# A hybrid decoder layer on one core: instructions put in another order at eight places

## The chip, the core and the metric

The kernel runs on one core of a Trainium2 chip. The metric is the device time of one execution in microseconds (us), the median of several. A profile is one execution that was traced; its times are read from the span's start. PE is the matrix engine (PEld its weight loads), DVE the vector engine, ACT the scalar engine, POOL GpSimd, SP the SyncE queue, from which every transfer of this kernel is issued.

## What is computed

One layer of a decoder with 1,040 positions (16 meta tokens and 1,024 real ones) of width 1,024, all in float32. Cut to what matters:

```python
xn   = rms_norm(h, mix_pre_g)
z, xbc, dt, q, k, v = split(xn @ w_in)
xbc  = silu(causal_dwconv(xbc, conv_w, conv_b))            # 4 taps along the tokens
y_ssd = rms_norm(ssd_scan(xbc, softplus(dt + dt_bias), a_log, d_skip) * silu(z), ssd_norm_g)
y_sb  = rms_norm(stick_breaking_attention(q, k, v), sb_norm_g)   # 16 heads
h   += rms_norm(concat(y_ssd, y_sb) @ w_out, mix_post_g)
gu   = rms_norm(h, ffn_pre_g) @ w_up
h   += rms_norm((gelu(causal_dwconv3(gu[:, :F])) * gu[:, F:]) @ w_down, ffn_post_g)
return h[16:]
```

Stick-breaking attention gives each key the weight beta times the product of (1 - beta) over the keys between it and the query, a scan along the keys. The state-space scan runs over chunks of 128 tokens.

## The kernel before

Every float32 product is done as three matmuls: an operand is split into a high part (ACT copies it to the reduced format) and a low part (POOL or DVE subtracts), and high x high, high x low and low x high are summed in PSUM. Large products are cut into 2x2 blocks and done in seven products of sums (Strassen's scheme), so that DVE and POOL form sums and PE does seven of eight parts.

The stages, in order of time:

- **Head** (to about 64 us): norm of x, its turn by PE, the first projections B0 and C0.
- **Projections** (64 to 374 us): thirteen `Duo`s, each two blocks of 128 output columns: x00, z00, x02, z02, bc, x10, z10, x12, z12 (names by group and block) and qk0 to qk3. A duo is seven products of 24 matmuls each (`product`, L298 to L321). The loop over `duos` (L739) emits product `m`, then a step of splitting the next duo's weights (`split_22`, `sums`, `split_3`, `split_1`, `split_4`), then the list `slots[j]` of what is left of the previous duo. For an x duo `conv_acts` (L489) makes these: four convolution taps on DVE, Silu on ACT (L502), the skip term on ACT with its store (`skip`, L506), and the turn to token order in three parts, each a transpose on PE into one of two PSUM banks (L481, L486) and a copy on ACT (L482, L487). `done_conv` (L521) says which of these stand in which slot. `dt_acts` does the same for the step sizes.
- **V** (374 to 455 us): the value projection.
- **Scan** (455 to 620 us): 18 units, one for each chunk and group (L1158). A unit loads what later units need (`load_zx` one ahead, `load_x` two, `load_bc` three), does its matmuls, and takes steps of the fill `qk_fill` (L908), the projections of q and k for heads 8 to 15. The evacuation `ev` (L915) of such a projection writes a tile `st` that is stored to DRAM (L921). `chunk_store` stores the result `zk` (L1119). At unit 2 two blocks of V's rows are copied from DRAM to DRAM (`vcd`, L1161).
- **Attention** (620 to 925 us): 64 steps, eight blocks of queries for each of eight pairs of heads (L1530). A step loads q three steps ahead, does the scores z, the sigmoid on ACT, the scan on DVE, and turns and mixes earlier blocks. Between them `some(n)` takes fill steps within a budget. `edge_mix` (L1321) ends a pair of heads and stores its tile `ysc` (L1329).
- **Output projection** (925 to 1,106 us): for each tile of 128 tokens two chains of 24 matmuls (`out_steps`, L1451), each evacuated by DVE (`ev2`, L1996) into a tile `mb`, then the two norms (`after`) and a turn of the result by PE with its copies and subtractions (`turn_x2`, L1714).
- **Feed forward** (1,106 us to the end): up products and down products.

The order within each engine is the order in which the code emits, under `manual_schedule`: for all five queues in the head, the scan and the attention, and for PE, DVE, ACT and POOL in the rest (in the output projection from its second tile on; there SP's order is the scheduler's). So an instruction that waits holds up everything behind it on its engine. The built program gives SP's transfers eight semaphores in turn: each transfer waits, beside what it needs, until the one eight places before it has landed.

Of the kernel before, what the change touches and what calls it, by code (L numbers as in the profile page):

```python
# [67 lines left out]
def tile_layer(ctx: ExitStack, tc: tile.TileContext, x, meta, rows, parts,  # L68
# [452 lines left out]
    def done_conv(duo, blocks):  # L521
        (a, ta_), (b, tb_) = (conv_acts(*args) for args in blocks)
        return [a[:2], a[2:], b[:2], ta_[:1] + b[2:], ta_[1:2], ta_[2:], tb_[:2], tb_[2:]]

# [207 lines left out]
    def merged(*lists):  # L732
# [3 lines left out]
    dts = dt_acts()  # L736
    slots = [b0_taps[:2] + dts[0], b0_taps[2:], c0_taps[:2], c0_taps[2:] + b0_turns[:1], b0_turns[1:2], b0_turns[2:],
             dts[1]]
    for i, q in enumerate(duos):  # L739
# [26 lines left out]
        slots = q.done(q)  # L766
        for acts_ in extra:
            slots[0] = acts_ + slots[0]
        if i == 1:
            slots = merged(slots, [[], dts[2], [], [], dts[3], [], dts[4]]) + [dts[5] + dts[6]]  # L770
        if i + 1 == n_early:
            t_stack.close()
            vl = v_stack.enter_context(tc.tile_pool(name="vl", bufs=1, side="left"))
            fetch_v(1, 0, vl)
# [131 lines left out]
    left, via_sbuf = [0], [0]  # L906

    def qk_fill():  # L908
        def chain(n, qs):
            which, p = qk_blocks[n]  # L910

            def ev(acc, c0, m):
                st = st_pool.tile([P, 2, CQ], F32R, tag="st", name=f"st{which}{p}{c0}")
                nc.scalar.activation(st[:, 0, :m], acc[:, :m], AF.Copy)
                if via_sbuf[0]:  # L915
                    raw = st_pool.tile([P, CQ], F32, tag="sw", name=f"sw{which}{p}{c0}", bufs=1)
                    nc.scalar.activation(raw[:, :m], acc[:, :m], AF.Copy)
                    nc.gpsimd.tensor_tensor(st[:, 1, :m], raw[:, :m], st[:, 0, :m].bitcast(F32), op=ALU.subtract)
                else:
                    nc.vector.tensor_tensor(st[:, 1, :m], acc[:, :m], st[:, 0, :m].bitcast(F32), op=ALU.subtract)  # L920
                nc.sync.dma_start(out=qkd[p][which][:, :, c0:c0 + m], in_=st[:, :, :m].bitcast(F32))  # L921

# [16 lines left out]

    def load_k(p):  # L940
        if p < 8:
            k = qkp.tile([P, 2, L], F32R, tag="k", name=f"k{p}")
# [32 lines left out]
    with tc.tile_pool(name="ssd", bufs=1, side="right") as sp:  # L975
# [125 lines left out]
        def chunk_store(g, c, em, xdt, yt, zk, xd, between):  # L1101
# [16 lines left out]
            nc.vector.tensor_tensor(zk[:, :, ts], xd[:, :, ts], zk[:, :, ts], op=ALU.mult)  # L1118
            nc.sync.dma_start(out=yd[c][:, 4 * g:4 * g + 4, :], in_=zk[:, :, ts])  # L1119

            def square():
                if g == 0:
                    squares[c] = sp.tile([P, 8, P], F32, tag="sqk", name=f"sqk{nm}")
                nc.scalar.activation(squares[c][:, 4 * g:4 * g + 4, ts], zk[:, :, ts], AF.Square)
# [33 lines left out]
        for n, (g, c) in enumerate(units):  # L1158
            if n == 2:
                for d, u in zip(vcd, (vd, vdp)):  # L1160
# [160 lines left out]
    def edge_mix(p, th):  # L1321
# [6 lines left out]
        nc.vector.tensor_tensor(tail, av.rearrange("p (t c) -> p t c", c=32), tail, op=ALU.add)  # L1328
        nc.sync.dma_start(out=yd1[:, :, p, :].rearrange("t d c -> d t c"), in_=ysc)  # L1329
        flat = ysc.rearrange("p t c -> p (t c)")  # L1330
# [199 lines left out]
    for step in range(8 * NT):  # L1530
# [8 lines left out]

        load_q(step + 3)  # L1540
        due = mix[:1]
        if len(turn) >= TURN_LAG:
            run(begin_turn())
        block = block_weights(p, i)
        next(block, None)
# [45 lines left out]
    do(4)  # L1591
    edge_mix(7, edge)
    run(meta_steps)
    while not closed[0]:
# [389 lines left out]
    for t in range(1, NT + 1):  # L1984
# [23 lines left out]
        steps = out_steps(1, t, wres2, ys.pop(0), ev2)  # L2008
        run(steps, 2)
        run(norm, 1)  # L2010
# [426 lines left out]
```

## Time and profile before

| | us |
|---|---|
| median of 3 runs | 1765.28 |
| lowest and highest run | 1764.16, 1766.97 |
| the profiled execution | 1767.73 |
| its span in the trace | 1766.0 |
| PE busy | 1686.9 |
| DVE, ACT, POOL busy | 1095.1, 741.1, 756.8 |
| transfers of the SP queue | 245.54 MB, 43.3% of 16 engines |

The page lists for each engine the busy time, then the span in 40 slices with the clock granted to PE, the chain of work that ended last, and the costliest groups of instructions, each with the idle time before it and what ended that. The trace answers further: who waited for whom, busy times by stretch, and instructions in order of time.

### The profile page before, as it was taken

The numbers are of one execution on the slowest core, as the hardware profiler recorded it, in microseconds if no ns is written. First come the engines' busy times: TensorE is split into PE (matmuls) and PEld (weight loads), VectorE is DVE, ScalarE is ACT, GpSimd is POOL, SyncE is SP. The second block draws the span as 40 slices with busy tenths as digits, with TensorE's granted clock in tenths as the row PEclk, the third lists the DMA queues.
The fourth block names the chain that finished last, engine by engine and source line by source line (L and its number), as shares of the span: only waits on it lengthen the run. The fifth ranks groups of instructions, "written<-read, shape, count | busy, mean of one in ns | idle before, by whom it ended". The sixth has DMA issues, their size and how long they took to land.

```text
span 1766.0 us, 29016 instructions
## 1 busy us (share of the span) xinstructions
PE 1686.9 (96%) x11508; PEld 1448.5 (82%) x11508; DVE 1095.1 (62%) x1279; ACT 741.1 (42%) x1110; POOL 756.8 (43%) x591
## 2 busy tenths in 40 slices
PE   6888999999999989899999989999999999999998
PEld 5888999987767777677777777989999988888887
DVE  7747444345256678787771366676666666658777
ACT  6443333322234455565553344543333333344544
POOL 4565666711265553223232211377777767500001
PEclk8999999999999989899999999999999999999999
DMA  5342344343487764534431754223233322196335
GB/s 194 130 135 85 121 132 136 135 153 116 153 231 231 222 185 132 163 110 115 118 94 67 245 167 143 72 94 125 93 108 95 115 90 90 67 323 224 102 104 189
DMA packets 164522, 247.40 MB, mean 140 GB/s; under 512 B 18489, under 2 KB 99489, under 8 KB 162706
## 3 DMA queue, kind: packets, MB, share of 16 engines
q1 hardware_dynamic: 164386, 245.54, 43.3%
q8 instruction: 91, 1.49, 0.4%
q14 instruction: 45, 0.37, 0.1%
HBM read 162.00 MB, written 83.47 MB: 139 GB/s over the span
## 4 chain that ended last, share of the span: by engine, by line
PE 74%; DVE 6%; issue 5%; ACT 3%; DMA 2%; POOL 1%; SPq 0%; POOLq 0%; DVEq 0%; ACTq 0%
PE fX L1841 10%; PE mo L1460 7%; PE dnA L2253 7%; PE fY L1841 6%; PE fA L1841 6%; PE dnB L2253 5%; PE av L1305 3%; PE z L1266 3%; PE tw L1287 3%; PE pj_q L219 2%; PE pj_k L219 2%; PE dXqk L309 2%; PE vB L812 2%; DVE kp L1270 2%; DVE cdX L498 1%
## 5 line engine op out<-in xcount | busy, mean ns | idle before, releaser
L1270 DVE TENSOR_TENSOR_SCAN kp<-kp,hold 128x344 f32<-128x344 f32 (+6 forms) x224 | 198.6, 946 | 45.5 <-ACT kp L1267 43.3
L183 POOL TENSOR_TENSOR wlo<-wr,whi 128x1024 fp32r<-128x1024 f32 x43 | 99.3, 2318 | 42.3 <-ACT whi L182 38.8
L2290 POOL TENSOR_TENSOR fms<-fms 128x1 f32<-128x1 f32 x8 | 2.3, 288 | 222.1 <-ACT dh L2175 195.8
L182 ACT ACTIVATE whi<-wr 128x1024 fp32r<-128x1024 f32 x43 | 45.7, 1062 | 112.2 <-PE fX L1841 76.2
L1913 DVE SCALAR_TENSOR_TENSOR ga<-gr,pp,ga 128x1024 f32<-128x1024 f32 x44 | 69.3, 1575 | 34.0 <-ACT ga L1906 33.3
L2175 ACT ACTIVATE dh<-ar 128x512 fp32r<-128x512 f32 x77 | 48.6, 631 | 94.9 <-PE dnB L2253 44.7
L1267 ACT ACTIVATE kp<-z 128x688 f32<-128x688 f32 (+6 forms) x112 | 78.9, 736 | 19.5 <-PE z L1266 18.6
L1266 PE MATMUL z<-k,q 64*128 64x348 f32 (+8 forms) x672 | 78.6, 356 | 5.8 <-ACT th L1292 3.9
L1287 PE MATMUL tw<-ident,kp 128*128 128x128 f32 x576 | 77.4, 280 | 6.0 <-DVE th L1290 3.1
L2176 DVE TENSOR_TENSOR dl<-ar,dh 128x512 fp32r<-128x512 f32 x77 | 53.2, 691 | 47.0 <-ACT dh L2175 47.0
L1305 PEld LDWEIGHTS av<-th,v 128*64 128x64 f32 x1152 | 62.4, 138 | 22.5 <-issue 11.7
L1245 POOL TENSOR_SCALAR cb<-kp 128x32 f32<-128x32 f32 x64 | 37.1, 583 | 99.9 <-DVE kp L1270 99.5
L1305 PE MATMUL av<-th,v 128*64 128x128 f32 x1152 | 78.0, 280 | 0.5 <-ACT ysc L1308 0.5
L1287 PEld LDWEIGHTS tw<-ident,kp 128*128 128x128 f32 x576 | 62.7, 142 | 15.9 <-issue 6.8
L1266 PEld LDWEIGHTS z<-k,q 64*128 64x128 f32 x672 | 54.7, 195 | 23.8 <-issue 10.1
L1292 ACT ACTIVATE th<-tw 128x1024 f32<-128x1024 f32 x64 | 55.3, 864 | 33.7 <-PE tw L1287 32.2
L2253 PE MATMUL dnA<-dl,dh 128*128 128x512 f32 x176 | 68.5, 389 | 0.0
L2253 PE MATMUL dnA<-dh 128*128 128x512 f32 x176 | 68.5, 389 | 0.0
L2253 PE MATMUL dnA<-dh,dl 128*128 128x512 f32 x176 | 68.5, 389 | 0.0
L1974 POOL TENSOR_TENSOR al<-wr,ah 128x512 fp32r<-128x512 f32 x20 | 28.6, 1431 | 77.5 <-ACT ah L1973 77.4
L1460 PE MATMUL mo<-wohb,yh 128*128 128x512 f32 x128 | 51.7, 404 | 6.3 <-DVE mb L1996 6.3
L2253 PE MATMUL dnB<-dh 128*128 128x512 f32 x132 | 51.3, 389 | 0.0
(999 smaller groups left out, 6080.5 us busy)
## 6 DMA issues: line engine op xcount, KB each, us to landing
wr<-in_w_up SPq DMA_DIRECT2D x44, 512.0 KB
fds<-ga SPq DMA_DIRECT2D x44, 256.0 KB
b<-in_w_down SPq DMA_DIRECT2D x44, 256.0 KB
ar<-fds SPq DMA_DIRECT2D x44, 256.0 KB
fda<-ga SPq DMA_DIRECT2D x33, 256.0 KB
ar<-fda SPq DMA_DIRECT2D x33, 256.0 KB
k<-qkd SPq DMA_DIRECT2D x8, 1040.0 KB
q<-qkd SPq DMA_DIRECT2D x64, 128.0 KB
```

What stands on the lines that cost most here:

```text
L183: nc.gpsimd.tensor_tensor(l, raw, h.bitcast(F32), op=ALU.subtract)
L219: mm(acc[:, :CQ - s], a[:, k, :], b[:, k % 4, c + s:c + CQ], start=(k == 0 and j == 0), stop=(k == KB - 1 and j == 2))
L1266: mm(z[:, j, :w], u[h, :], r[h, a:a + w], start=s_ == 0, stop=s_ == 2)
L1267: nc.scalar.activation(kp[:, :, a:a + w], z[:, :, :w], AF.Sigmoid, scale=-QSCALE)
L1270: nc.vector.tensor_tensor_scan(part, part, hold[:, L - n + a:L - n + a + w][:, ::-1], 1.0 if ci == 0 else kp[:, j, a + w:a + w + 1], op0=A ...
L1287: nc.tensor.transpose(tw[:, j, b, :], bt[:, j, c0:c0 + P], ident)
L1292: copied[0] = nc.scalar.activation(th[:, :, :nb, :], tw[:, :, :nb, :], AF.Copy, scale=-1.0, bias=1.0).ins
L1305: mm(av[halves[j], :], v[:, kb, halves[j]], th[:, j, b, :], start=kb == 0, stop=kb == i)
L1460: recent[0] = mm(acc, u[:, k, :], v[:, cs], start=(k == 0 and j == 0), stop=(k == 7 and j == 2))
L1841: mm(acc[:, c, :nn], u[:, k, :], v[:, k, c0:c0 + nn], start=first and k == 0 and j == 0, stop=k == 3 and j == 2, skip_group_check=not first)
L1913: nc.vector.scalar_tensor_tensor(v, self.g[jj][:, :, i:i + 256], fconv_w[:, j, i:i + 1], v, op0=ALU.mult, op1=ALU.add)
L2253: mm(banks[BANK[n], t], u[:, 0, c], v[:, 1, :], start=(n in (1, 2, 5) and p == 0 and i == 0), stop=(p == NPR - 1 and i == 2), skip_group_c ...
```

## The change

Eight edits of order; no instruction is added or taken away, and POOL's order is the same.

1. `done_conv` lists a duo's Silu and skip one product later, and the turns of both blocks one product each, so that the last three turn parts of an x duo fall into the first three slots of the duo after the next. The step sizes' parts `dts` move with them, and the pool of the turned tiles closes one duo later.
2. `qk_fill`: the store of `st` is put on a list `stores` and issued at the start of the next evacuation, or by `load_k`.
3. `chunk_store`: the store of `zk` is issued with the square of the same unit, one unit later.
4. The copies `vcd` are issued at unit 12, not 2.
5. `edge_mix`: the store of `ysc` goes on the same list, and the list is emptied at step 6 of each pair too.
6. Step 0 of the attention takes its five fill steps ahead of its first scores.
7. Output projection: four steps of a tile's chains (a whole first chain with its evacuation) go ahead of the norm's steps and the turn, where there were two (half a chain).
8. The two extra slots at the end of a duo's list go to the next duo's slots 0, 1, 2 in turn, not all to slot 0.

```diff
@@ done_conv
-        return [a[:2], a[2:], b[:2], ta_[:1] + b[2:], ta_[1:2], ta_[2:], tb_[:2], tb_[2:]]
+        return [a[:2], a[2:4], a[4:] + b[:2], b[2:4], ta_[:1] + b[4:], ta_[1:2], ta_[2:], tb_[:1], tb_[1:2], tb_[2:]]
@@ first slots
-    slots = [b0_taps[:2] + dts[0], b0_taps[2:], c0_taps[:2], c0_taps[2:] + b0_turns[:1], b0_turns[1:2], b0_turns[2:],
-             dts[1]]
+    slots = [b0_taps[:2] + dts[0], b0_taps[2:4], b0_taps[4:] + c0_taps[:2], c0_taps[2:4], c0_taps[4:] + b0_turns[:1],
+             b0_turns[1:2], b0_turns[2:], dts[1]]
@@ loop over duos
-        for acts_ in extra:
-            slots[0] = acts_ + slots[0]
+        for k, acts_ in enumerate(extra):
+            slots[k] = acts_ + slots[k]
         if i == 1:
-            slots = merged(slots, [[], dts[2], [], [], dts[3], [], dts[4]]) + [dts[5] + dts[6]]
-        if i + 1 == n_early:
+            slots = merged(slots, [[], dts[2], [], dts[3], [], [], dts[4]]) + [dts[5], dts[6]]
+        if i == n_early:
@@ qk_fill, load_k
+    stores = []
+    def put_stores():
+        while stores:
+            dst, src = stores.pop(0)
+            nc.sync.dma_start(out=dst, in_=src)
             def ev(acc, c0, m):
+                put_stores()
...
-                nc.sync.dma_start(out=qkd[p][which][:, :, c0:c0 + m], in_=st[:, :, :m].bitcast(F32))
+                stores.append((qkd[p][which][:, :, c0:c0 + m], st[:, :, :m].bitcast(F32)))
     def load_k(p):
+        put_stores()
@@ chunk_store
-            nc.sync.dma_start(out=yd[c][:, 4 * g:4 * g + 4, :], in_=zk[:, :, ts])
             def square():
+                nc.sync.dma_start(out=yd[c][:, 4 * g:4 * g + 4, :], in_=zk[:, :, ts])
@@ units
-            if n == 2:
+            if n == 12:
                 for d, u in zip(vcd, (vd, vdp)):
@@ edge_mix
-        nc.sync.dma_start(out=yd1[:, :, p, :].rearrange("t d c -> d t c"), in_=ysc)
+        stores.append((yd1[:, :, p, :].rearrange("t d c -> d t c"), ysc))
@@ attention steps
         load_q(step + 3)
+        if n == 6 or (p, n) == (6, 3):
+            put_stores()
...
+        if step == 0:
+            some(5)
         block = block_weights(p, i)
@@ output projection
-        run(steps, 2)
+        run(steps, 4)
         run(norm, 1)
```

What this makes of three queues follows. First ACT in the projections, in duo z00, while x00's convolution is being finished: `cdX` is a block's Silu, `craw_x` its skip term, `craw_z` the evacuation of product 2, `whi1x` and `whi4x` the high parts of the next duo's weights, `xtkX` the copies of turned parts. Before:

```order
L502 ACTIVATE cdX_1185<-cdX_1185 128x1040
L508 ACTIVATE craw_x_841<-cdX_1185,pp 128x1040
L318 ACTIVATE craw_z_1114<-dAz_1088 128x520
L182 ACTIVATE whi1x_1251<-wrx_812 128x8x128
L487 ACTIVATE xtkX_1217<-tt_X_1_1255 128x512
L182 ACTIVATE whi4x_1286<-s24x_1149 128x8x128
L487 ACTIVATE xtkX_1217<-tt_X_2_1290 128x512
L482 ACTIVATE xtkX_1323<-tt_X_0_1324 16x128
```

The same place now:

```order
L318 ACTIVATE craw_z_1100<-dAz_1074 128x520
L182 ACTIVATE whi1x_1244<-wrx_812 128x8x128
L482 ACTIVATE xtkX_1248<-tt_X_0_1249 16x128
L502 ACTIVATE cdX_1185<-cdX_1185 128x1040
L508 ACTIVATE craw_x_841<-cdX_1185,pp 128x1040
L182 ACTIVATE whi4x_1280<-s24x_1149 128x8x128
L487 ACTIVATE xtkX_1248<-tt_X_1_1284 128x512
L487 ACTIVATE xtkX_1248<-tt_X_2_1315 128x512
```

The second block's Silu and skip have moved behind the evacuation, `whi1x` and the first turned part; `whi4x` and the other two parts still stand behind them.

Second SP in the scan at unit 2: `yd` is a unit's stored result, `vcd` the copies of V's rows, `bt`, `ct`, `bn` the state's next chunks, `zk` and `xd` what unit 3 needs, `sl` and `sg` what unit 5's decays need. Before:

```order
L1119 DMA yd_90<-zk_0_4663 128x4x2
L1161 DMA vcd_3897<-vd 8x16384
L1161 DMA vcd_3898<-vd 8x16384
L989 DMA bt_4464<-bcd_529 128x256
L990 DMA ct_4465<-bcd_530 128x256
L993 DMA bn_4466<-bnd_533 128x256
L989 DMA bt_4467<-bcd_531 128x256
L990 DMA ct_4468<-bcd_532 128x256
L993 DMA bn_4469<-bnd_534 128x256
L1028 DMA zk_1_4827<-zd_115 128x4x128
L1028 DMA xd_1_4829<-xdd_102 128x4x128
```

The same place now:

```order
L913 DMA qkd_544<-st_4729 256x1x260
L998 DMA bt_4464<-bcd_529 128x256
L999 DMA ct_4465<-bcd_530 128x256
L1002 DMA bn_4466<-bnd_533 128x256
L998 DMA bt_4467<-bcd_531 128x256
L999 DMA ct_4468<-bcd_532 128x256
L1002 DMA bn_4469<-bnd_534 128x256
L1037 DMA zk_1_4823<-zd_115 128x4x128
L1037 DMA xd_1_4825<-xdd_102 128x4x128
```

The two copies are gone from here (they stand eight and nine places ahead of `xk_7` at unit 12 now), and the store of unit 1's result has moved behind unit 2's loads.

Third DVE in the output projection, tile 4: `mb<-mo_4_0` and `mb<-mo_4_1` are the evacuations of its two chains, `b11l` and `b21l` the subtractions of tile 2's turn, `oxn` and `mo` the ends of two norms (tile 3's and that of the two last meta rows). Before:

```order
L1726 TENSOR_TENSOR b11l<-x2tp_10851,b11h 128x4x128
L1726 TENSOR_TENSOR b21l<-x2tp_10851,b21h 128x4x128
L1712 SCALAR_TENSOR_TENSOR oxn_10813<-mb_10725,rs_ff_10847,gffn 128x1024
L1712 SCALAR_TENSOR_TENSOR mo_10484<-mb_10483,rs_ff_10867,gffn 2x1024
L1996 SCALAR_TENSOR_TENSOR mb_10830<-mo_4_0_10834,r_sb,mb_10830 128x512
L1996 SCALAR_TENSOR_TENSOR mb_10830<-mo_4_1_10885,r_sb,mb_10830 128x512
```

The same place now:

```order
L2010 SCALAR_TENSOR_TENSOR mb_10830<-mo_4_0_10834,r_sb,mb_10830 128x512
L1740 TENSOR_TENSOR b11l<-x2tp_10864,b11h 128x4x128
L1740 TENSOR_TENSOR b21l<-x2tp_10864,b21h 128x4x128
L1726 SCALAR_TENSOR_TENSOR oxn_10813<-mb_10725,rs_ff_10860,gffn 128x1024
L1726 SCALAR_TENSOR_TENSOR mo_10484<-mb_10483,rs_ff_10880,gffn 2x1024
L2010 SCALAR_TENSOR_TENSOR mb_10830<-mo_4_1_10885,r_sb,mb_10830 128x512
```

The first chain's evacuation has moved ahead of the turn's and the norms' work.

More of the change, by code (lines that the diff above doesn't have):

```diff
@@ L1592, in tile_layer @@
     edge_mix(7, edge)
+    put_stores()
     run(meta_steps)
```

## The prediction

> **What bounds the kernel now.** I read the page first, then busy times by stage, then the waits of PE, then the stretches in which its clock was low, and last the rows around each wait in order of time. The page's first part:
>
> ```profile
> PE 1686.9 (96%) x11508; PEld 1448.5 (82%) x11508; DVE 1095.1 (62%) x1279; ACT 741.1 (42%) x1110; POOL 756.8 (43%) x591
> ```
>
> PE is busy for 1,686.9 of 1,766.0 us of span, so nothing but PE's remaining 79 us, and the time that it runs at a lower clock, is to be had by reordering. Busy times by stage (columns: stretch, length, PE, PEld, DVE, ACT and POOL busy with counts, granted clock, DMA share, GB/s), for the projections, scan, attention and output projection:
>
> ```profile
> 64.00:374.00 310.00, 288.27 (x2334) 284.16 (x2332) 154.62 (x149) 119.10 (x161) 183.81 (x107) 0.98 0.37 126
> 455.00:620.00 165.00, 157.92 (x1124) 126.05 (x1122) 91.42 (x142) 63.80 (x94) 88.07 (x81) 0.96 0.73 211
> 620.00:925.00 305.00, 289.82 (x2674) 222.68 (x2674) 236.54 (x286) 169.13 (x273) 104.16 (x126) 0.96 0.46 132
> 925.00:1106.00 181.00, 173.24 (x944) 137.21 (x944) 81.64 (x97) 69.64 (x109) 38.59 (x49) 0.99 0.46 152
> ```
>
> PE is short of its stage by 21.7, 7.1, 15.2 and 7.8 us, and the clock is under 1.00 in each. The rest of the span (head, V, feed forward) keeps its order. What PE waited for (total us, times, longest):
>
> ```profile
> PE mo L1460 <- DVE mb L1996: 6.3, 5, 4.0
> PE tt_X L481 <- ACT xtkX L487: 6.1, 4, 1.7
> PE tt_X L486 <- ACT xtkX L487: 4.6, 4, 1.2
> PE z L1266 <- ACT th L1292: 3.9, 3, 3.4
> PE tt_B L486 <- ACT xtkB L482: 3.2, 1, 3.2
> ...
> PE sg L1042 <- DMA sg<-diagd: 2.7, 1, 2.7
> ...
> PE pj_k L219 <- ACT sw L917: 2.2, 1, 2.2
> ...
> PE tt_X L481 <- ACT cdX L502: 1.8, 1, 1.8
> PE dAz L309 <- POOL wlo1z L183: 1.8, 1, 1.8
> PE pz L674 <- DVE s L667: 1.7, 1, 1.7
> ```
>
> The clock has a second price. Seven stretches, each beginning 1 to 5 us after one of these waits, ran at a granted 0.50:
>
> ```profile
> 119.40:126.20 6.80, 5.81 (x27) 5.82 (x28) 0.00 (x0) 1.66 (x4) 3.48 (x4) 0.50 0.59 155
> 146.70:150.10 3.40, 3.40 (x18) 3.40 (x17) 0.59 (x3) 0.19 (x2) 0.00 (x0) 0.50 0.01 2
> 245.70:249.10 3.40, 3.40 (x18) 3.40 (x17) 0.00 (x0) 0.00 (x0) 1.12 (x3) 0.50 0.98 262
> 508.50:515.30 6.80, 5.92 (x25) 4.47 (x26) 3.09 (x5) 2.17 (x4) 4.48 (x5) 0.50 0.97 285
> 628.00:634.80 6.80, 6.80 (x32) 6.05 (x34) 4.67 (x7) 0.41 (x1) 1.49 (x2) 0.50 0.76 209
> 737.20:744.00 6.80, 6.49 (x40) 4.34 (x40) 6.13 (x8) 4.25 (x8) 2.64 (x3) 0.50 0.75 223
> 1054.60:1058.00 3.40, 3.40 (x10) 2.65 (x9) 2.27 (x3) 1.05 (x2) 0.79 (x2) 0.50 0.50 136
> ```
>
> At half the clock, PE loses half of such a stretch: in order 3.4, 1.7, 1.7, 3.4, 3.4, 3.4, 1.7 us. Not every wait is followed by one, so I count the clock at half of that where a wait goes.
>
> **A. Projections (edits 1 and 8).** Who holds up the turns `tt_X`? DVE, ACT and POOL in duo z10, and its second product in the chain of waits:
>
> ```profile
> 234.66 3.96 DVE L498 SCALAR_TENSOR_TENSOR cdX<-craw_x,pp,cdX 128x1040 f32<-128x1040 f32 x2
> ```
> ```profile
> 238.65 1.07 ACT L502 ACTIVATE cdX<-cdX 128x1040 f32<-128x1040 f32 x1 [5.03 <-DVE cdX L498]
> 239.75 1.17 ACT L508 ACTIVATE craw_x<-cdX,pp 128x1040 f32<-128x1040 f32 x1
> ```
> ```profile
> 241.31 1.05 ACT L182 ACTIVATE whi1x<-wrx 128x1024 fp32r<-128x1024 f32 x1
> ```
> ```profile
> 244.56 2.18 POOL L183 TENSOR_TENSOR wlo4x<-s24x,whi4x 128x1024 fp32r<-128x1024 f32 x1
> ```
> ```profile
> 223.01 2.88 PE dXz L309 x24
> ```
>
> ACT stands 5.03 us in front of the second block's Silu, and what is behind it, the evacuation of a product, `whi1x` and the first block's turned copies, comes after Silu and skip; PE has two PSUM banks for turns and waits. After the change the Silu waits as long, but the evacuation, `whi1x` and a turned copy stand ahead of it, and the last turns fall a duo later, where nothing is waited for. So all `tt_X` waits go, and with the copies and splits ahead of the tap waits `wlo1z`, `pz` and `tt_B` too: 6.1 + 4.6 + 3.2 + 1.8 + 1.8 + 1.7 = 19.2 us, and the clock's 3.4 + 1.7 + 1.7 = 6.8. What is late next is `whi4x`, now right behind Silu and skip, and `wlo4x` behind it, which the next duo's second product needs. Taps end at 238.6 less the 1.8 of `wlo1z`, so 236.8; Silu, skip and `whi4x` (as long as `whi1x`) make that 240.1, POOL's 2.18 makes it 242.3. The next duo's second product comes a duo after the one at 223.0: less the 1.8, plus seven products of 2.88 and about 1.5 for the turns, an estimate, 242.9. It fits by some 0.6 us. That is thin over five such duos, so I take three quarters of the waits, 14.5 us, and 3.4 of clock: **17.9**.
>
> **B. Scan (edits 2, 3, 4).** SP around unit 2, and the copy in the chain of waits:
>
> ```profile
> 496.77 0.43 SPq L993 DMA_DIRECT2D bn<-bnd  x1
> 499.44 0.37 SPq L1028 DMA_DIRECT2D zk<-zd  x1
> ```
> ```profile
> 492.73 9.13 DMA vcd<-vd
> ```
>
> The loads `zk` and `xd` stand eight places behind the two copies, and their semaphores are the copies': SP stops from 497.20 to 499.44 and again ahead of `xd`. `sg` is behind these, and PE's 2.7 us behind `sg`. With the copies at unit 12 this goes, with 0.9 more just behind it in the next small gap, 3.6 in all, and 3.4 of clock. At unit 12 the places eight behind are `xk` for two units on and a `qkd` store, wanted a unit (165 / 18 = 9.2 us) later; I charge 1 us there, between 0 and 3.6. Taken: 0.8 x 3.6 + 1.5 - 1 = **3.4**.
>
> **C. First scores (edit 6).** In the chain, then ACT:
>
> ```profile
> 620.04 3.82 DMA yd<-zk
> ```
> ```profile
> 625.32 2.03 ACT L1267 ACTIVATE kp<-z 128x688 f32<-128x688 f32 x3
> 627.22 0.41 ACT L914 ACTIVATE st<-pj_k 128x260 fp32r<-128x260 f32 x1
> ```
>
> ACT's sigmoids wait for the last `yd` store to land at 623.9, then the evacuation of `pj_k` comes behind them, and PE has no bank: 2.2 us. Now the fill's chain and its evacuation come first. The sigmoids do not come sooner, so DVE's scans begin as before. I take 1.3 of the 2.2, since PE reaches the first scores later by what the fill takes and may then wait there, and half of the clock's 3.4: **3.0**.
>
> **D. `wor` for a pair's end (edits 2 and 5).** SP, then the chain:
>
> ```profile
> 727.12 0.56 SPq L921 DMA_DIRECT2D qkd<-st  x1
> ...
> 729.64 0.47 SPq L1378 DMA_DIRECT2D wor<-in_w_out  x1
> ```
> ```profile
> 729.64 5.74 DMA wor<-in_w_out
> ```
>
> The store of `st` waits for its tile, and `wor` is issued 2.5 us behind it, lands at 735.4, ACT's copy of it stands ahead of `th`, and PE's scores wait 3.4 us for that. With the store put off, `wor` can be issued up to 3.1 us earlier. Taken: 0.75 x 3.1 + half of the clock's 3.4, less rounding: **3.9**.
>
> **E. Output projection (edit 7).** DVE at tile 4:
>
> ```profile
> 1051.83 1.27 DVE L1712 SCALAR_TENSOR_TENSOR mo<-mb,rs_ff,gffn 2x1024 f32<-2x1024 f32 x1
> 1053.03 1.39 DVE L1996 SCALAR_TENSOR_TENSOR mb<-mo,r_sb,mb 128x512 f32<-128x512 f32 x2
> ```
>
> The evacuation that frees the chain's bank (`mo` <- `mb`, 6.3 us of waits in all) is behind two norms. With the evacuation ahead of turn and norms, the bank is free a chain earlier, and DVE, busy for 81.64 of this stage's 181 us, has room for the rest during the second chain. What could be late is the turn's subtractions, needed by no PE work within a tile. Taken: 5.4 of the 6.3, and half of 1.7: **6.2**.
>
> The sum is 17.9 + 3.4 + 3.0 + 3.9 + 6.2 = 34.4. Counted against the profiled execution (1,767.73, span 1,766.0, so 1.7 around it), that gives 1,733.3; it lies 2.45 above the median of the runs, 1,765.28, so the forecast is 1765.3 - 34.4, about **1,731 us**. With every wait and clock share in full the gain is 19.2 + 3.6 + 2.2 + 3.4 + 6.3 = 34.7 and 6.8 + 3.4 + 3.4 + 3.4 + 1.7 = 18.7, so 1,712. With half of the taken, 1,748.
>
> **The rivals.** First, the half-clock stretches are not caused by the short waits and stay, in A, B and C. Then 3.4 + 1.5 + 1.7 = 6.6 of the sum goes: 1,738. For it speaks that the two waits of over 3 us, `z` and `mo`, are both followed by a stretch, and not all short ones are; against it, that the stretch at 146.70 follows a single wait of 1.7. Chance 0.20. [...]
>
> Second, `wlo4x` is late: the 0.6 us of A are not there because DVE's taps end later. PE then waits 2 to 3 us at the second product of five duos (POOL's 2.18 stands whole in the way): 13 us less, 1,744. It decides once taps end 0.6 us later than I reckon. Chance 0.20.
>
> Third, slower. A unit's load of `zk` reuses the tile of three units before, and its store, moved a unit later, now stands right ahead of it on SP, so SP waits for that landing in every unit.
>
> A unit's nine issues on SP at about 0.43 (the `bn` row of B) are some 4 us; with a landing of 3.8 (the `yd` row) 7.8 of the unit's 9.2, which fits. With a landing like the 9.13 of `vcd` it is 13.1, 3.9 too long, over 13 units 51 us: 1,782. It decides against the gain from a landing of 7.8 us. The scan's DMA share of 0.73 speaks for slower landings, but 256 KB rows here are far under `vcd`'s size. Chance 0.08.
>
> Fourth, nothing to measure: PE's waits turn up elsewhere in the same length, because another engine, DVE above all, sets the pace (it is busy 237 of 305 us in the attention); 1,764. Chance 0.06.
>
> **How the numbers follow.** My forecast has 0.46. It, the first and the second rival are all faster: 0.86. Slower 0.08, same 0.06, where 0.2% is 3.5 us, about what this kernel's measurement tells from none. The range leaves out the third and fourth rival and the ends of the full and the half sum: 1,716 to 1,750.
>
> **What would show it.** In the changed kernel's profile: the waits of `tt_X`, `tt_B` and `pz` gone from PE's list and the stage from 64 us on shorter by 15 to 20; clock 1.00 where 0.50 stood; ACT's 5 us in front of Silu still there; SP without a stop ahead of `zk` and `xd` at unit 3; `wor` issued earlier; `mo` <- `mb` near zero. Wrong if PE waits for `wlo4x`, if SP waits long for `yd` stores in each unit, or if 310, 165, 305 and 181 us shrink by less than half of the terms.

## The result, and the profile after

The changed kernel takes 1738.7 us (median of four runs, 1736.3 to 1741.0) beside 1766.1 for the kernel before (four runs): a ratio of 0.984 (95% interval 0.9814 to 0.9866), so 27 us less. The forecast was 1,731 us, 34 less, in a range of 1,716 to 1,750. The profiled execution of the changed kernel was the fastest of its four (span 1734.6 us), so the two traces lie 31.4 us apart. One run of the experiment `u_zk` below, 2052.5 us at a granted clock of 0.748, was in a slow state and is left out of its figures.

First the four stages in which PE waited, before and after. A stage begins at the same instruction in both kernels: the first product of a duo, the first product of V (which ends the projections), the first decay product of the scan, the last turn of the scan, the meta keys' product that ends the attention, and the first `fX` product of the feed forward, so that the last stretch also holds the first 53 us of the feed forward. (Columns as in the prediction.) The kernel before:

```profile
64.10:374.00 309.90, 288.17 (x2333) 284.06 (x2331) 154.62 (x149) 119.10 (x161) 183.81 (x107) 0.98 0.37 126
464.90:618.10 153.20, 147.92 (x1053) 116.94 (x1053) 87.10 (x134) 59.38 (x86) 86.70 (x80) 0.96 0.75 217
618.10:924.60 306.50, 291.10 (x2686) 223.75 (x2683) 237.74 (x287) 169.27 (x273) 105.12 (x127) 0.96 0.46 132
924.60:1158.60 234.00, 226.24 (x1295) 185.78 (x1296) 118.27 (x132) 98.52 (x145) 58.55 (x64) 0.99 0.41 136
```

The changed kernel:

```profile
61.90:359.30 297.40, 284.45 (x2333) 281.27 (x2331) 156.24 (x149) 120.20 (x161) 188.23 (x107) 0.99 0.38 132
451.30:603.80 152.50, 146.62 (x1051) 116.14 (x1052) 87.24 (x134) 58.19 (x84) 87.12 (x79) 0.97 0.75 218
603.80:902.30 298.50, 284.57 (x2685) 218.65 (x2683) 239.12 (x287) 170.16 (x275) 114.07 (x128) 0.99 0.46 134
902.30:1127.10 224.80, 223.46 (x1296) 185.16 (x1297) 118.94 (x132) 98.17 (x145) 58.74 (x64) 1.00 0.43 143
```

Divided into what PE idled (the time in which neither a matmul nor a weight load ran) and what the half clock took (half of every stretch at 0.50), the two traces read (half is an estimate, a little high for these: in the kernel before a matmul of a product, L309, starts 0.12 us after the one before it at a granted 1.00 and 0.217 at 0.50, one of `mo`, L1460, 0.229 and 0.427, which makes 45 and 46% of a stretch):

| stage | forecast | length | idle before, after | half clock before, after |
|---|---|---|---|---|
| head | 0 | -2.2 | 19.6, 18.9 | 6.8, 3.4 |
| projections (A) | -17.9 | -12.5 | 20.8, 12.0 | 6.8, 3.4 |
| V | 0 | +1.1 | 1.4, 1.7 | 0, 0 |
| scan (B) | -3.4 | -0.7 | 5.2, 5.8 | 6.8, 5.1 |
| attention (C, D) | -6.9 | -8.0 | 14.5, 13.0 | 11.9, 3.4 |
| output projection (E), to the first `fX` | -6.2 | -9.2 | 7.6, 1.3 | 1.7, 0 |
| the rest of the feed forward | 0 | +0.1 | 0, 0 | 0.7, 1.0 |

(The idle time leaves out what follows PE's last instruction and the waits that end right where a stage begins, 9.4 us in each trace.) Of the 31.4 us, then, 16.5 are idle time of PE (forecast 25) and 18.5 are clock (forecast 9), less 3.5 in which PE was busy longer. The head's 3.4 us of clock have nothing to do with the change, whose first instruction stands behind it.

This split is that of one run, and its clock was lucky. The changed kernel's other three runs had a granted clock of 0.986, 0.985 and 0.985, where this one had 0.991: by their spans, an estimate, 24 to 26 us lost to the half clock and not 16. Nine runs of the kernel before, taken with the first experiments, had 0.980 to 0.984, in the middle 0.982, or 32 us. So in a usual run the clock gives some 7 us of the 27, and about 20 come from elsewhere, for the most part idle time. Eight of the twelve later traces have a half-clock stretch of 6.8 us at the end of the attention, which neither of these two has.

PE's waits between 62 and 359 us of the changed kernel, to be held against the waits of `tt_X`, `tt_B`, `wlo1z` and `pz` in the prediction:

```profile
PE dXx L309 <- DVE craw_x L321: 3.9, 2, 3.1
PE dXx L309 <- POOL craw_x L230: 2.3, 2, 1.3
PE pz L674 <- DVE s L667: 1.7, 1, 1.7
PE dXz L309 <- POOL wlo4z L183: 1.5, 1, 1.5
PE dXqk L309 <- POOL wlo4qk L183: 1.3, 1, 1.3
PE dYx L309 <- POOL wlo3x L183: 1.0, 1, 1.0
PE tt_X L481 <- ACT xtkX L487: 0.4, 2, 0.2
```

The turns' waits are gone to 0.4 us, as forecast; `pz` stands as it stood; one wait of 3.1 us for DVE is new; and four new waits of 1.1 to 1.5 us are there, all at the second product of a duo. Two are put down to POOL's `craw_x` (L230), two memsets of 0.34 us together that only come last of what is waited for. POOL in duo x12 shows the rest:

```profile
233.39 2.19 POOL L183 TENSOR_TENSOR wlo4x<-s24x,whi4x 128x1024 fp32r<-128x1024 f32 x1 [4.43 <-ACT whi4x L182]
235.51 0.34 POOL L230 MEMSET craw_x<- 128x3 f32 x2
```

and ACT ahead of it:

```profile
230.09 1.07 ACT L502 ACTIVATE cdX<-cdX 128x1040 f32<-128x1040 f32 x1 [3.78 <-DVE cdX L498]
231.20 1.17 ACT L508 ACTIVATE craw_x<-cdX,pp 128x1040 f32<-128x1040 f32 x1
232.27 1.04 ACT L182 ACTIVATE whi4x<-s24x 128x1024 fp32r<-128x1024 f32 x1
```

ACT still stands in front of the Silu, 3.78 us, and `whi4x` is behind Silu and skip. `wlo4x` ends at 235.58, and PE, which reads it with the product's third matmul, has waited for 1.09 us:

```profile
235.63 0.39 PE L309 MATMUL dXx<-t2h,wlo4x 128*128 128x260 f32 x1 [1.09 <-POOL craw_x L230]
```

That is the second rival's mechanism, at less than half its price in idle time. Its condition holds too: the taps end later than the prediction reckoned. The last tap ahead of that Silu and POOL's `wlo1x`, in the kernel before:

```profile
237.31 1.30 DVE L498 SCALAR_TENSOR_TENSOR cdX<-craw_x,pp,cdX 128x1040 f32<-128x1040 f32 x1
242.43 2.17 POOL L183 TENSOR_TENSOR wlo1x<-wrx,whi1x 128x1024 fp32r<-128x1024 f32 x1 [6.25 <-ACT whi1x L182]
```

In the changed kernel:

```profile
226.93 3.12 DVE L498 SCALAR_TENSOR_TENSOR cdX<-craw_x,pp,cdX 128x1040 f32<-128x1040 f32 x1
226.24 2.72 POOL L183 TENSOR_TENSOR wlo1x<-wrx,whi1x 128x1024 fp32r<-128x1024 f32 x1 [0.44 <-ACT whi1x L182]
```

With `whi1x` ahead of the Silu, POOL's `wlo1x` runs beside the last tap, and the tap takes 3.12 us where it took 1.30. It is so at all four late duos (3.12 or 3.13 us now, 1.30 before), and 1.8 us is more than the 0.6 that the prediction had to spare.

`wor`, at the first pair's end in the attention, is issued earlier:

```profile
707.53 0.34 SPq L1387 DMA_DIRECT2D wor<-in_w_out  x1
```

This is 0.8 us behind PE's wait of 1.5 us for `th` at that place (it ends at 706.72); in the kernel before it was 3.9 us behind the same wait (729.64, and 725.70), so the 3.1 us of step D are there. In the output projection PE waits for `mb` no more.

SP in the scan shows what the third rival described:

```profile
SPq L1037 <- DMA yd<-zk: 31.6, 12, 4.8
```

SP waits in 12 units for the store right ahead of the load of `zk`. At the end of the scan ACT pays for it:

```profile
597.84 0.39 ACT L922 ACTIVATE st<-pj_k 128x260 fp32r<-128x260 f32 x1 [5.45 <-DMA qkd<-st]
```

### The profile page after: what moved, and what is told of

The parts are those of the page before. It is cut to its first block, busy times and chain, and to the rows that moved or that the text cites. A ratio compares the mean times of both kernels' runs of the same rounds, so it can differ in the third digit from the quotient of the medians.

```text
span 1734.6 us, 29010 instructions
## 1 busy us (share of the span) xinstructions
PE 1672.1 (96%) x11508; PEld 1438.2 (83%) x11508; DVE 1098.9 (63%) x1279; ACT 741.5 (43%) x1110; POOL 768.1 (44%) x591
## 4 chain that ended last, share of the span: by engine, by line
PE 75%; DVE 5%; issue 4%; ACT 3%; POOL 2%; DMA 2%; SPq 0%; DVEq 0%; POOLq 0%; ACTq 0%
PE fX L1855 10%; PE mo L1469 10%; PE dnA L2267 7%; PE fY L1855 7%; PE fA L1855 7%; PE dnB L2267 5%; PE av L1314 3%; PE z L1275 2%; DVE kp L1279 2%; PE pj_k L219 2%; PE tw L1296 2%; PE dXqk L309 2%; PE vB L812 2%; PE pj_q L219 2%; PE dYqk L309 1%
## 5 line engine op out<-in xcount | busy, mean ns | idle before, releaser
L183 POOL TENSOR_TENSOR wlo<-wr,whi 128x1024 fp32r<-128x1024 f32 x43 | 99.3, 2319 | 41.0 <-ACT whi L182 37.5
L1314 PEld LDWEIGHTS av<-th,v 128*64 128x64 f32 x1152 | 62.3, 138 | 22.4 <-issue 11.5
L2267 PE MATMUL dnB<-dh,dl 128*128 128x512 f32 x132 | 51.3, 389 | 0.0
```

The source lines that it names most:

```text
L183: nc.gpsimd.tensor_tensor(l, raw, h.bitcast(F32), op=ALU.subtract)
L1314: mm(av[halves[j], :], v[:, kb, halves[j]], th[:, j, b, :], start=kb == 0, stop=kb == i)
L2267: mm(banks[BANK[n], t], u[:, 0, c], v[:, 1, :], start=(n in (1, 2, 5) and p == 0 and i == 0), stop=(p == NPR - 1 and i == 2), skip_group_c ...
```

## The experiments

The theory to be tested is the prediction's: each edit's gain is the waits of PE that leave its own stage, with the half-clock stretches behind them. Against it stand that waits only move to a later stage, and that the clock goes by chance. Each ratio is to runs of the kernel before that were taken together with the experiment's, with its 95% interval. The kernel before has medians of 1765.4 to 1769.1 in these sets, so between sets the ratios are the fairer comparison: a difference of 0.001 is 1.8 us.

| kernel | median us | ratio to before | PE idle | half clock |
|---|---|---|---|---|
| changed | 1738.7 | 0.984 (0.9814 to 0.9866) | 52.6 | 16.4 |
| u_proj | 1749.9 | 0.9911 (0.9898 to 0.9925) | 59.5 | 24.8 |
| u_out | 1746.3 | 0.9892 (0.9879 to 0.9906) | 54.7 | 27.7 |
| u_zk | 1736.2 | 0.9831 (0.9817 to 0.9844) | 49.0 | 22.4 |
| whi4first | 1731.4 | 0.9803 (0.9789 to 0.9816) | 46.5 | 21.1 |
| u_fill | 1735.4 | 0.9816 (0.979 to 0.9842) | 49.3 | 22.6 |
| u_stores | 1740.0 | 0.9846 (0.9821 to 0.987) | 53.4 | 22.7 |
| u_vcd | 1738.9 | 0.9837 (0.9811 to 0.9863) | 52.0 | 21.0 |
| best_a | 1725.4 | 0.9763 (0.9738 to 0.9787) | 41.1 | 17.5 |
| best_b | 1722.4 | 0.9744 (0.9724 to 0.9763) | 40.8 | 15.9 |
| best_c | 1720.5 | 0.9747 (0.9726 to 0.9768) | 38.2 | 15.8 |
| gap_short | 1736.6 | 0.9832 (0.9811 to 0.9854) | 50.7 | 14.7 |
| gap_mid | 1755.8 | 0.9938 (0.9912 to 0.9963) | 59.5 | 24.1 |

(Idle and half clock, in us, are of the one profiled execution of each, from the span's start to its end, the idle time less the 9.4 us as above.)

**u_proj: the projections as before.** The edit puts back the lists of `done_conv`, the first slots and the loop's `extra`:

```diff
-        return [a[:2], a[2:4], a[4:] + b[:2], b[2:4], ta_[:1] + b[4:], ta_[1:2], ta_[2:], tb_[:1], tb_[1:2], tb_[2:]]
+        return [a[:2], a[2:], b[:2], ta_[:1] + b[2:], ta_[1:2], ta_[2:], tb_[:2], tb_[2:]]
```

> The changed kernel with edits 1 and 8 undone, all else kept. Theory (each edit's gain is the PE waits that leave its own stage, with the half-clock stretches behind them): PE's idle time between the first duo and V goes from 12.0 back to about 20.8 us and the half clock there from 3.4 to 6.8 us, so about 12 us longer than the changed kernel's 1738.7: 1751, and the waits of tt_X, tt_B and wlo1z are in PE's list again. Rival (a wait removed early only moves the wait to a later stage): 1739 to 1742.

Measured 1749.9, 11.2 above the changed kernel (12.5 by the ratios). The stage's idle time is 20.8 us, its half clock 6.8, its length 310.0 (309.9 before), and the waits are the old ones:

```profile
PE tt_X L481 <- ACT xtkX L487: 6.0, 4, 1.7
PE tt_X L486 <- ACT xtkX L487: 4.6, 4, 1.2
PE tt_B L486 <- ACT xtkB L482: 3.2, 1, 3.2
```

The theory holds: the projections are worth 11 to 12 us by themselves, and no later stage gives that back.

**u_out: edit 7 undone.**

```diff
-        run(steps, 4)
+        run(steps, 2)
```

> The changed kernel with edit 7 undone. Theory: PE waits 6.3 us for the evacuations mo<-mb again and has one half-clock stretch (1.7 us) behind the long one: 8 us longer, 1746.7. Rival (the output stage got shorter because the attention left its work in another state, not by the edit): 1739 to 1741.

Measured 1746.3, 7.6 above (9.2 by the ratios). The wait is back:

```profile
PE mo L1469 <- DVE mb L2010: 6.1, 5, 3.8
```

In this profile the wait of 3.8 us is followed by a half clock of 6.8 us. The theory holds.

**u_zk: the store of `zk` in its own unit.**

```diff
+            nc.sync.dma_start(out=yd[c][:, 4 * g:4 * g + 4, :], in_=zk[:, :, ts])
             def square():
-                nc.sync.dma_start(out=yd[c][:, 4 * g:4 * g + 4, :], in_=zk[:, :, ts])
```

> The changed kernel with edit 3 undone: the store of zk is issued in its own unit again, so that SP no longer waits for its landing right behind its issue. In the changed kernel SP stands 31.6 us in 12 places for that. Theory (these waits delay the stores of st at the end of the scan, and ACT and PE there: waits of 2.0, 1.0, 0.8 and 0.8 us from 597 to 610 us): 3 to 5 us shorter, 1734 to 1736. Rival (SP is ahead of PE by more than it waits, nothing of it reaches PE): 1738 to 1740.

Measured 1736.2, 2.5 below the changed kernel (1.6 by the ratios, whose intervals overlap). The stage itself, in the profile, is 149.1 us long and not 152.5, PE's idle time there 3.3 and not 5.8, and the waits at its end are down to two of 0.8. So edit 3, as made, cost the scan 3.4 us in the traces; how much of that reaches the median these runs don't resolve.

**whi4first: `whi4x` ahead of the second Silu.**

```diff
-        return [..., ta_[:1] + b[4:], ta_[1:2], ta_[2:], ...]
+        return [..., ta_[:1], b[4:] + ta_[1:2], ta_[2:], ...]
```

> The changed kernel with the second block's Silu and skip one product later still, behind whi4x and ahead of the second turned part. Theory (PE's four waits of 1.1 to 1.5 us at the second product of a duo are for wlo4x, late because ACT makes whi4x only behind Silu and skip): these waits go, 4 to 5 us shorter, 1734. Rival (ACT's order only moves the wait: the turned copies or the next duo's evacuation come later by as much, and tt_X waits): 1738 to 1741.

Measured 1731.4, 7.4 below the changed kernel (6.5 by the ratios) and more than expected. The projections:

```profile
61.80:350.90 289.10, 281.67 (x2333) 279.90 (x2332) 155.16 (x149) 121.13 (x161) 191.37 (x107) 0.99 0.39 136
```

They take 289.1 us and not 297.4. All four waits at second products are gone, 5.5 us of idle time, and a half-clock stretch is 3.4 us shorter (it begins at 97 us here and at 87 us there, in both ahead of the waits that the edit takes away, so that is not the edit's doing). No `tt_X` wait has come in their place. So the order on ACT is enough to bring `wlo4x` in time, although the taps are as slow as before; what it would be with fast taps and the old order was not tried.

**u_fill: edit 6 undone.**

```diff
-        if step == 0:
-            some(5)
```

> The changed kernel with edit 6 undone: step 0 of the attention does its first scores ahead of the five fill steps again. Theory (the evacuation of pj_k behind the sigmoids kept PE waiting 2.2 us, with a half-clock stretch of 6.8 us behind it): PE's wait for sw of over 2 us is back, and a stretch at 0.50 within 5 us of it; 3 to 6 us longer, 1742 to 1745. Rival (the wait only moves, since the first scores now wait in the fill's place): 1738 to 1740.

Measured 1735.4, not above the changed kernel: the theory's time fails here. There is a wait of PE for `sw`, of 1.33 us and not 2.2, with a half-clock stretch of 3.4 us behind it. In the changed kernel two waits of 0.8 for `sw`, one of 0.97 and one of 1.35 for DVE's `th` stand in its place:

```profile
PE tw L1296 <- DVE th L1299: 2.9, 3, 1.4
...
PE pj_k L219 <- ACT sw L925: 1.6, 2, 0.8
PE tw L1296 <- ACT sw L925: 1.0, 1, 1.0
```

The attention is 299.5 us with the edit undone and 298.5 with it, its idle time 10.9 and 13.0, its half clock 6.8 and 3.4. Edit 6 moved waits, it took none away; what it saved in these two traces is clock, and the medians show nothing of that.

**u_stores: edits 2 and 5 undone.**

```diff
-                stores.append((qkd[p][which][:, :, c0:c0 + m], st[:, :, :m].bitcast(F32)))
+                nc.sync.dma_start(out=qkd[p][which][:, :, c0:c0 + m], in_=st[:, :, :m].bitcast(F32))
```

> The changed kernel with the stores of st and ysc issued where they are made (edits 2 and 5 undone). Theory (the store of st stands ahead of wor on SP at the first pair's end, and PE waits for the copy of wor): the wait of 3.4 us of z for th at about 715 us is back with a half-clock stretch of 6.8 us, 4 to 7 us longer, 1743 to 1746. Rival (wor is early enough by the other edits): 1738 to 1740.

Measured 1740.0, 1.3 above, and the ratios' intervals overlap. The profile tells why it may be so little. Scan and attention:

```profile
448.80:596.60 147.80, 145.16 (x1051) 114.29 (x1052) 88.81 (x134) 59.54 (x86) 89.84 (x80) 0.98 0.76 220
596.60:904.10 307.50, 289.48 (x2685) 223.29 (x2683) 236.70 (x287) 169.41 (x273) 104.66 (x127) 0.96 0.46 135
```

The attention is 9.0 us longer than in the changed kernel, and `z` waits for `th` again:

```profile
PE z L1275 <- ACT th L1301: 4.0, 3, 3.5
```

So the mechanism of D is as forecast: this wait of 3.5 us is back, with a half-clock stretch of 6.8 us. It is not all of the 9.0, though. PE also waits 3.2 us for `sw` at the attention's start, with another stretch of 6.8 us behind it, because ACT there waits for a store of `st`:

```profile
PE pj_k L219 <- ACT sw L925: 4.0, 2, 3.2
```
```profile
600.85 0.39 ACT L922 ACTIVATE st<-pj_q 128x260 fp32r<-128x260 f32 x1 [4.51 <-DMA qkd<-st]
```

In the changed kernel ACT has such a wait a little sooner, at the scan's end (the row at 597.84), and the scan is 4.7 us longer there. So the wait is in part only moved: what the scan loses by the late stores, the attention's start partly gains. The two stages together are 4.3 us longer with the edits undone.

**u_vcd: edit 4 undone.**

```diff
-            if n == 12:
+            if n == 2:
```

> The changed kernel with edit 4 undone: the copies vcd at unit 2 again. Theory (zk and xd stand eight places behind the copies and wait for their landing, sg behind them): SP waits about 4 us for vcd at unit 2, PE 2.7 us for sg, and a half-clock stretch of 6.8 us follows: 4 to 7 us longer, 1743 to 1746. Rival (with the stores put off SP is ahead enough to bear the wait): 1737 to 1740.

Measured 1738.9, no different. SP waits for the copies again, 3.6 us, and PE waits once, now for `yt` and not for `sg`:

```profile
PE yt L1122 <- DVE yt L1097: 2.8, 1, 2.8
```

DVE stands there behind an evacuation for which ACT waited for a store of `st`:

```profile
506.32 0.39 ACT L922 ACTIVATE st<-pj_q 128x260 fp32r<-128x260 f32 x1 [8.25 <-DMA qkd<-st]
```

Against that, the waits of 2.0 and 1.0 us at the end of the scan are not there. That the copies at unit 12 slow the stores at the end of the scan would explain these; it was not tried by itself. The scan's length is 153.8 beside 152.5.

**best_a: four waits taken at their places.** On the changed kernel: the edits of whi4first and u_zk, and

```diff
-             b0_taps[4:] + c0_taps[:2], c0_taps[2:4], c0_taps[4:] + b0_turns[:1],
+             b0_taps[4:] + c0_taps[:2], c0_taps[2:3], c0_taps[3:] + b0_turns[:1],
...
-            slots = merged(slots, [[], dts[2], [], dts[3], [], [], dts[4]]) + [dts[5], dts[6]]
+            slots = merged(slots, [[], dts[2], [], dts[3], [], [], []]) + dts[4:]
```

> Four edits on the changed kernel: the second Silu and skip behind whi4x (as in whi4first, 1731.4), the store of zk in its own unit (as in u_zk), the last tap of C0 one slot later, so that DVE's sum of a product is not behind it (PE waits 3.1 us at 85 us), and the first decay product of the step sizes in the next duo's first slot, so that PE does not wait 1.6 us for DVE at 141 us. Theory (waits that are removed in different stages add up): 1731.4 less 2.5, less 2 to 3 with up to 3.4 of clock, less 1.6: 1721 to 1725. Rival (PE meets the next limit, DVE or POOL, right behind each): 1728 to 1731.

Measured 1725.4, between the two expectations and just outside the theory's. The projections came to 284.1 us, 13.4 less than in the changed kernel, with 2.8 us of idle time and no half clock at all. So the reductions within that stage add up, and its clock came with them. The wait of 3.1 us at 85 us was DVE's: two taps of C0 stood ahead of the sum that frees PE's accumulator (changed kernel):

```profile
82.96 4.54 DVE L498 SCALAR_TENSOR_TENSOR cdC<-craw_C,pp,cdC 128x1040 f32<-128x1040 f32 x2
87.42 0.69 DVE L321 TENSOR_TENSOR craw_x<-dXx,craw_x 128x520 f32<-128x520 f32 x1
```

With one tap behind the sum 0.9 us of it are left.

**best_b: stores of `st` put off only where that pays.**

```diff
-                stores.append((qkd[p][which][:, :, c0:c0 + m], st[:, :, :m].bitcast(F32)))
+                pair = (qkd[p][which][:, :, c0:c0 + m], st[:, :, :m].bitcast(F32))
+                if via_sbuf[0]:
+                    stores.append(pair)
+                else:
+                    nc.sync.dma_start(out=pair[0], in_=pair[1])
```

> best_a with the stores of st issued where they are made during the scan, and put off only from the last unit on, so in the attention. Theory (putting them off costs the scan: with them undone it was 4.6 us shorter, and gains in the attention, by wor): the scan of best_a, 148.4 us, falls by 0 to 1 since the store of zk is already undone there, and the attention keeps its 299: 1723 to 1726. Rival (the two undone stores cost the scan separately): 1720 to 1722.

Measured 1722.4, between the theory's 1723 and the rival's 1722. The scan is 147.4 us (148.4 in best_a), as the theory had it, the attention 299.8 (299.2). The intervals of best_a and best_b overlap, so that this edit gains anything is not shown.

**best_c: without edit 6.** Its edit to best_b is that of u_fill.

> best_b with edit 6 undone, so the attention's first scores ahead of its five fill steps again. In u_fill this came out 3 us below the changed kernel, but in runs of another chip's set. Theory (edit 6 takes the wait of 2.2 us out and puts two of about 1 us and one of 1.35 in): the attention from 299.8 to about 298, PE idle there down by 2 us, 1719 to 1721. Rival (the difference was between the sets of runs): 1721 to 1724.

Measured 1720.5, with a ratio of 0.9747 beside best_b's 0.9744: no difference. The median is in the theory's range, but best_b's would be too on this set: 0.9744 of its 1765.6 is 1720.4. In the profile the attention's idle time fell by 2.6 us, as the theory had it, but its half clock rose by 3.4, and it is 300.2 us long and not 298. So the rival holds.

**gap_short and gap_mid: which waits a half clock follows.** Both are best_b with eight waits added to PE in the last duos, where best_b has no half clock between 64 and 438 us; the numbers of copies are 1 and 3. The function that makes a wait (the eight places that use it are left out here):

```diff
+    def pe_gap(nm):
+        t1, t2 = psum_mm(f"ga{nm}"), psum_mm(f"gb{nm}").rearrange("p (a b) -> p a b", b=P)
+        mm(t1[:, :16], ident, ident[:, :16], start=True, stop=True)
+        nc.scalar.activation(gap[:, 0:16], t1[:, :16], AF.Copy)
+        for r in range(3):
+            nc.scalar.activation(t2, ident.unsqueeze(1).to_broadcast([P, 4, P]), AF.Copy)
+        nc.scalar.activation(gap[:, 16:32], t1[:, :16], AF.Copy)
+        mm(t1[:, 32:48], ident, gap[:, 16:32], start=True, stop=True)
```

> best_b with eight added waits of PE in the last duos, 8.7 us and more apart, in a stretch that had no half clock and hardly a wait: PE writes a small product, ACT reads it and makes one 128x512 copy, PE reads what ACT made. About 1.5 us of idle PE each. Theory (the clock is halved after a window of 3.41 us on a fixed grid in which PE idles for about 1.8 us or more): no half-clock stretch in the stretch of the last duos, or one at most; 12 us longer than best_b. Rival (any wait of over 1 us can halve the clock, by chance): two to four stretches, 17 to 22 us longer. [...]

> The same with three copies, so about 2.7 us of idle PE each. Theory (a window of 3.41 us with 1.8 us of idle): a wait of 2.7 leaves 1.8 or more in one window at about three of four places on the grid, so about 6 of the 8 are followed by a half-clock stretch of 3.4 or 6.8 us, and which ones can be read off the grid; 22 us of waits and 10 to 20 us of clock longer than best_b. Rival (any wait over 1 us, by chance): no more stretches than in gap_short. [...]

In gap_short the waits came out at 0.9 to 1.3 us, and none of the eight was followed by a half clock:

```profile
PE ga L589 <- ACT gap L588: 8.6, 8, 1.3
```

In gap_mid they are 2.1 to 2.5 us, and five of eight were:

```profile
PE ga L589 <- ACT gap L588: 18.2, 8, 2.5
```

In both traces, as in all others, every change of the clock lies on one grid of 3.41 us (from 294.4 to 369.5 us in gap_mid are 22 steps of it). Along that grid, the windows that hold most of a wait, and two that follow one, read (second number PE's busy time of the 3.40; the wait at 317 us is split over the two windows from 314.90 on):

```profile
277.30:280.70 3.40, 1.77 (x16) 1.68 (x15) 0.00 (x0) 1.64 (x4) 2.08 (x1) 1.00 0.67 221
291.00:294.40 3.40, 0.99 (x8) 1.00 (x9) 0.00 (x0) 3.34 (x8) 0.45 (x1) 1.00 0.00 0
294.40:297.80 3.40, 3.40 (x18) 3.40 (x18) 1.37 (x1) 1.38 (x2) 3.24 (x3) 0.50 0.60 243
304.60:308.00 3.40, 1.70 (x14) 1.70 (x15) 0.18 (x1) 2.53 (x5) 0.72 (x1) 1.00 0.16 67
308.00:311.40 3.40, 3.40 (x19) 3.40 (x18) 0.00 (x0) 0.45 (x1) 1.47 (x1) 0.51 0.02 5
314.90:318.30 3.40, 2.21 (x20) 2.12 (x18) 0.70 (x1) 1.35 (x4) 2.19 (x1) 1.00 0.00 0
318.30:321.70 3.40, 2.45 (x20) 2.46 (x21) 0.00 (x0) 0.86 (x3) 0.00 (x0) 1.00 0.00 0
328.50:331.90 3.40, 1.31 (x11) 1.31 (x12) 0.94 (x2) 2.93 (x6) 2.62 (x3) 1.00 0.02 8
342.20:345.60 3.40, 2.12 (x17) 2.12 (x18) 0.00 (x0) 2.14 (x4) 1.16 (x2) 1.00 0.51 154
352.40:355.80 3.40, 1.27 (x12) 1.17 (x11) 0.88 (x2) 2.94 (x6) 0.00 (x0) 1.00 0.69 281
366.10:369.50 3.40, 1.34 (x11) 1.34 (x12) 0.41 (x1) 2.89 (x7) 0.00 (x0) 1.00 0.00 0
```

Both kernels are longer than best_b by about what was expected, 14 and 33 us. The four windows in which PE was busy for 1.34 us or less are each followed by a half-clock window, as is that with 1.70; those with 1.77, 2.12, 2.21 and 2.45 are not. Of waits of nearly one length (2.1 to 2.5 us) some are followed by a half clock and some are not; in these rows what tells them apart is how much of a wait falls into one window: 1.70 us of idle time and more where a half clock follows, 1.63 and less where none does. The rival fails: by it, gap_mid would have had no more stretches than gap_short.

Counted over all 14 traces, from 60 us on, of the windows at full clock in which PE ran no matmul for at least 1.8 us, 42 of 43 were followed by a half clock; of those with 1.6 to 1.8, 9 of 23; with 1.2 to 1.6, 9 of 66; with 0.9 to 1.2, 2 of 81. Another 29 half-clock stretches, of 91 in all, began behind windows with less than 0.9 us, most of them in the attention and at its end; what sets those off, these runs don't show.

## Why the prediction was right, and where its steps were not

**The whole.** Direction and size came out, 27 us of a forecast 34, but all three of the signs that the prediction named for being wrong are there: PE waits for `wlo4x`, SP waits for a `yd` store in 12 units, and the scan shrank by less than half of its term. The time is also what the first rival gave (1,738), but not by its mechanism: the half-clock stretches behind the turns, `sg`, `z` and `mo` did go with their waits, though the scan kept 5.1 of its 6.8 us of half clock and a new stretch came in A. In a usual run, by the estimate above, the clock gave some 7 us where the sum had 9, and the rest about 20 where its idle time had 25. In the traces A and B fell short of their terms, and the attention and E came out over theirs, so the total is nearer than its parts.

Undone one part at a time (u_proj, u_out, u_zk, u_fill, u_stores, u_vcd), the edits give back some 15 us of the 27 (16.5 by the ratios), all of it by A and E. Undoing any one part of edits 2 to 6 costs nothing clear, though scan and attention together are 8.7 us shorter in the two traces. They were not undone together, so what they are worth as a group is open.

**A** was mis-sized: 12.5 us in the trace and 11.2 by u_proj, not 17.9. The clock came out as taken, 3.4; the idle time fell by 8.8 us and not 14.5. The step that failed is "it fits by some 0.6 us" for `wlo4x`: it was 1.1 to 1.5 us late at four duos, 5 us in all. The step took over the end of the taps from the trace before; but the last tap now runs beside POOL's `wlo1x`, which the same edit moved, and takes 1.8 us longer. whi4first shows that `whi4x` behind the Silu is what makes that matter; that the slower tap used up the margin is read from the rows, no run took it away by itself. Of "all waits go" `pz` did not, and the 3.2 us of `tt_B` came back as 3.1 at the next product, whose accumulator DVE had not freed; best_a, which moves what DVE does there, has no wait of `pz` and 0.9 us of the other. The second rival was right on the place and on the condition, and about twice too dear (13 us, where whi4first gained 7.4).

**B** gave 0.7 us, not 3.4. The wait for `sg` went, as the step said, but the two edits that came with it took it back: the store of `zk` a unit later holds SP 31.6 us (the third rival's mechanism, which cost the scan 2.5 us of idle time and not 51, since the waits for landings were 4.8 us at most and SP is mostly ahead), and late stores of `st` hold its tiles. The prediction charged 1 us for unit 12 alone.

**C** was wrong: "the evacuation comes first" is so, but PE then waits as long for `sw` and `th` behind the scores. The step took 1.3 us as the part of the idle time that would stay gone; in u_fill and best_c the attention has 2.1 and 2.6 us less of it without the edit. Its clock is there in the traces (3.4 us less with the edit, in both pairs), but the medians show no gain.

**D** was right in its mechanism (`wor` is issued 3.1 us ahead, `z`'s 3.4 us are gone, and in u_stores' trace 3.5 us of wait and 3.4 of clock are back, against 3.9 in the sum), but the store's other effect, in the scan, was not in the sum, and the median moved by 1.3 us only.

**E** was under-sized: 9.2 us in the trace and 7.6 by u_out, where the sum took 6.2 and the full price was 8.0. There was no reason in the rows to take less than the full wait.

**The clock.** "Half of the stretch behind each wait that goes" was a guess about chance. In gap_mid, of eight waits of 2.1 to 2.5 us five were followed by a half clock, those with 1.70 us and more of idle time in one window of the grid; in gap_short, of eight waits of 0.9 to 1.3 us none was. By the counts over all traces, an estimate, the 1.7 us waits of the turns were at the edge (9 of 23 windows with 1.6 to 1.8 us), `mo`, with 4.0 us, was certain, `z`, with 3.4, nearly, and `sg`, with 2.7, likely.

## What to carry to other kernels

A step that is put behind an engine's wait should be the one that nobody needs soon: moving one instruction (`whi4x` ahead of a Silu) gave 7.4 us more beside the 11.2 of the projections' whole reordering. An engine's time for an instruction was not a constant here: ask what will run beside it in the new order (a tap took 1.30 us, and 3.12 beside POOL's subtraction). When a wait is taken away, look in the same trace for what the waiting engine would have met a microsecond later, on every engine; and undo each edit of a bundle by itself, since two of these eight (the later stores of `zk`, the fill ahead of first scores) gave nothing or took. best_c, without them and with the other moves of best_a and best_b, is 1720.5 us, 18 below the changed kernel. Before a trace is split into causes, hold its granted clock against that of the other runs. Here the waits of PE worth cutting first were those that leave 1.6 us and more of idle time in one window: 51 of 66 such windows were followed by a half clock, and 9 of 66 with 1.2 to 1.6 us.

## What the runs showed of the hardware

In all 14 traces the granted clock changes on a grid of 3.41 us that runs through the whole trace and stands at another place from trace to trace (first record of the clock from 13.3 to 18.1 us after the start of the span; 13.6 in the kernel before, 15.6 in the changed one). The more PE idled within one window of the grid at full clock, the more often a half clock followed: 42 of 43 windows with 1.8 us and more, 9 of 23 with 1.6 to 1.8, 2 of 81 with 0.9 to 1.2. That is not all of it, since 29 of 91 stretches began behind windows with less than 0.9 us. In gap_mid five of eight waits of 2.1 to 2.5 us had a half clock behind them. The granted clocks of one kernel's runs go with their times (the kernel before: 0.985 at 1759.2 us, 0.978 at 1774.4); why they differ from run to run was not shown, since only one run of each kernel was traced.

A tap on DVE (L498, 128x1040) took 1.30 us where POOL did nothing, and 2.6 to 3.1 us where it began beside POOL's subtraction of a low part (L183), in the kernel before as in the changed one.
